# Two chained transformer blocks on one NeuronCore: the first modulation in column tiles of TensorE, constant-tile products spread behind four of its sums

## The chip, the cores and the metric

The kernel runs on one core of a Trainium2 chip. The metric is device time in microseconds of one execution, as the median of several runs. The engines are TensorE (PE in the profile, its weight loads PEld), VectorE (DVE), ScalarE (ACT), GpSimd (POOL) and SyncE (SP, which here only issues DMAs).

## What is computed

Two residual blocks over a sequence of 512 tokens of width 1024. The part that matters here is the head of the first block: a conditioning vector `c` (1024 values) is multiplied with `w_ada`, and the six parts of the result shift, scale and gate the two halves of the block. The first two parts, shift and scale, are needed before anything else can be multiplied:

```python
mod = c @ w_ada[layer] + b_ada[layer]
sh_a, sc_a, gt_a, sh_m, sc_m, gt_m = jnp.split(mod, 6, axis=-1)
h = modulate(rmsnorm(x, g_mix[layer]), sh_a, sc_a)   # rmsnorm(x) * (1 + sc_a) + sh_a
z = h @ w_in[layer]
```

Everything else (three kinds of attention, two feed-forward parts, a state-space mixer) comes after `z` and isn't touched.

## The kernel before

The activations lie transposed, features on the 128 partitions and the 512 tokens along the free axis: eight channel tiles of 128x512. All large products are made from rounded halves: each operand is split into a high part (`hh`, `wh`) and a low part (`hl`, `wl`), and three matmuls of the type fp32r (`wh·hh`, `wh·hl`, `wl·hh`) give one product. Plain f32 matmuls are used for small sums; each of those is two matmul instructions in the trace.

The program doesn't issue instructions at once. It records operations through `Rec`, and `Plan.schedule` (a list scheduler) then decides the order on each engine from estimated costs (`Plan.price`) and estimated DMA landings. Each engine takes, among the operations that are ready by the estimate, the one recorded first. On TensorE one rule is added: the estimate counts 0.2 us (`SWITCH`) for a change between tile shapes, and if the first candidate has another tile shape than the last matmul, a ready one of the same shape is preferred as long as it was recorded within the next 120 operations (`STAY`). The chip then runs each engine's list strictly in that order.

The start of the kernel goes like this:

- `warm(30)` issues 30 products of a constant tile `wt` with itself (128x512, fp32r), which nobody reads. They keep TensorE active while the first loads land.
- SP loads the eight tiles of `x` (`xT`), then the modulation's weights. For each channel tile `j` four DMAs bring `aw[j, 0..3]` (256 KB each), which hold `w_ada` for eight blocks `k` of 128 inputs and 256 outputs: 128 for the shift, 128 for the scale of channel tile `j`. Between them go the first pieces of `w_in` (`wr0` to `wr3`, 512 KB each).
- `SumSq` and `rstd_sb` make the row norm `R0`: squares on ACT, sums on DVE, four sums over partitions on TensorE, a power on POOL, a transpose that spreads it on TensorE (`T<-ident,rs`), a copy on ACT.
- `ada0_vec(j)` multiplies five of the eight blocks on DVE: one `tensor_scalar` and four `scalar_tensor_tensor` of 128x256 that accumulate into `aacc`. `ada0_sum(j)` does the other three on TensorE, with the weight block as the stationary operand and one column of `c` as the moving one (`S<-vec,aw`), and adds the column sums of `aacc` with a column of ones (`S<-ones,aacc`). Both accumulate in one PSUM bank; then ACT writes the shift (`mod`) and DVE the scale (`ca`).
- `h_tile(j)` makes the modulated tile: DVE multiplies `xT` with `ca` and `R0`, ACT adds the shift and rounds (`hh`), DVE makes the rest (`hl`).
- The first product, job 0 (`linT4`), accumulates four output tiles at once in four PSUM banks (two of tag `mm`, one `O`, one `S`). For each `k` from 0 to 7 it runs `start_step(k)`, which loads weights for tile `k + 5` and makes sum and modulated tile `k + 1`, and then 12 matmuls of 128x512 with tile `k`: 96 matmuls in all.
- After `ada0_vec(0)` stands `warm(18)`: 18 more products of the constant tile. A copy of a piece of `aacc` into `wt` just before makes them wait for that accumulation.

The tag `S` has three PSUM banks. One is an output bank of job 0 for its whole length, so two sums of the modulation can be under way at a time.

Of the kernel before, what the change touches and what calls it, by code (L numbers as in the profile page):

```python
# [10 lines left out]
F32 = mybir.dt.float32  # L11
F32R = mybir.dt.float32r
I32 = mybir.dt.int32
AF = mybir.ActivationFunctionType
OP = mybir.AluOpType
# [35 lines left out]
class Plan:  # L51
# [78 lines left out]
    def price(self, o, name, out, aps):  # L130


        free = lambda x: x.free_size() if callable(x.free_size) else x.free_size
        n = max([free(x) for x in aps]) if aps else 1
        ps = any(x.space == PSUM for x in aps)
        o.port, o.mode = False, None
        if name == "dma_start":
            sz = 4
            for d in out.shape:
                sz *= d  # L140
            o.nbytes = sz
            return 0.6 if o.eng == "POOL" else 0.06
        if o.eng == "PE":
            l, r = o.a[1], o.a[2]
            m, cut = free(l), lambda v: 32 if v <= 32 else 64 if v <= 64 else 128
            o.mode = (cut(l.ap[0][1]), 128 if name == "transpose" or r.dtype == F32R else cut(m))
            if name == "transpose":
                return 0.108
            if r.dtype == F32R:
                return max(0.11, free(r) / 2400.0 + 0.0136)  # L150
            return 2 * max(0.111 if m > 64 else 0.055 if m > 32 else 0.03,
                           (free(r) / 1200.0 + 0.005) * (1.0 if m > 32 else 0.4))
        if o.eng == "ACT":
            c = n / 1200.0 + (0.052 if ps else 0.093)
            if name == "activation" and (hasattr(o.kw.get("scale"), "tensor") or hasattr(o.kw.get("bias"), "tensor")):
                c += 0.093
            if o.kw.get("accum_out") is not None:
                c += 0.093
            return c
        ins = [x for x in aps if x is not out and x is not o.kw.get("accum_out")]  # L160
        big = [x for x in ins if free(x) > 8 and x.space != PSUM]
        two = name in ("tensor_scalar", "tensor_copy") and not ps
        if o.eng == "DVE":
            if name == "memset":
                return 0.01 + n / 960.0
            o.port = len(big) > 1 or (two and len(big) == 1)
            c = 0.069
            if name in ("tensor_scalar", "scalar_tensor_tensor"):
                c += 0.06 * sum(free(x) == 1 for x in ins)
            return c + n / (1920.0 if two else 960.0)  # L170
        if name == "memset":
            return 0.04 + n / 1200.0
        o.port = True
        if name == "tensor_copy":
            return 0.06 + n / 1040.0
        return 0.1 + n / 355.0 if name == "tensor_scalar" else 0.95 if n <= 8 else 0.15 + n / 475.0
# [347 lines left out]
def tile_kernel(ctx: ExitStack, tc: tile.TileContext, A, out):  # L524
    nc = tc.nc
    plan = Plan(nc)
    act, dve, pe, gp, sp = (Rec(plan, e) for e in ("ACT", "DVE", "PE", "POOL", "SP"))
# [21 lines left out]
    def nm(s):  # L549
        uid[0] += 1  # L550
        return f"{s}_{uid[0]}"

    def slot(dt=F32, name="a"):
        return plan.tile(ar, NA, [128, T], dt, "a", nm(name))
# [8 lines left out]
    def bank(tag):  # L563
        n = {"S": 3, "O": 1}.get(tag, 2)
        return plan.tile(psp[tag], n, [128, T], F32, tag, nm(tag))
# [7 lines left out]
    def mm(o, l, r, start, stop):  # L573
        pe.matmul(o, l, r, start=start, stop=stop, skip_group_check=True)
# [15 lines left out]
    def V(name):  # L590
        a, b = VEC[name]
        return vec[:, a:b]

    ones = cst.tile([128, 1], F32, name="ones")
# [3 lines left out]
    mod = cst.tile([128, 48], F32, name="mod")  # L598
    ca = cst.tile([128, 32], F32, name="ca")
# [52 lines left out]
    def rstd_sb(acc, n, tag="T"):  # L652
        p = spread(rstd_of(acc, n, tag), tag)
        R = slot(F32, "R")
        act.copy(R, p)
        return R
# [119 lines left out]
    cT = V("c")  # L776
# [127 lines left out]
    def comp_mlp(which):  # L904
        def body(ids):
# [54 lines left out]
    z = lambda j, ev: linT([wi[j, 0], wi[j, 1]], 4, 8, H1, ev)  # L960
    linT4([[wi[j, i] for i in range(2)] for j in range(2)], 4, 8, H1, [z_evac("kcvc"), z_evac("kskw")],
          pre=lambda k: start_step(k))
    z(4, z_evac("q")(0))
    beside([A["w_ck1"][i] for i in range(4)], comp_mlp("k"), 8.0)
# [484 lines left out]
    wt = slot(F32R, "warm")  # L1449
# [3 lines left out]
    def warm(n):  # L1453

        for _ in range(n):
            mm(wp, wt[:, 0:128], wt, True, True)
    warm(30)
    for i in range(8):
        x1[i] = slot(F32, "xT")
        sp.dma_start(x1[i], A["xT"][i])  # L1460
    aw = {}

    def ada0_load(j):
        for i in range(4):
            aw[j, i] = slot(F32, "aw")
            sp.dma_start(aw[j, i], A["w_ada0"][j, i])

    acc0 = {}
    KD = 5

    def ada0_vec(j):

        acc = slot(F32, "aacc")
        w = lambda k: aw[j, k // 2][:, 256 * (k % 2):256 * (k % 2) + 256]
        dve.tensor_scalar(acc[:, 0:256], w(0), cT[:, 0:1], None, op0=OP.mult)
        for k in range(1, KD):
            dve.scalar_tensor_tensor(acc[:, 0:256], w(k), cT[:, k:k + 1], acc[:, 0:256], op0=OP.mult, op1=OP.add)
        acc0[j] = [(w(k), cT[:, k:k + 1]) for k in range(KD, 8)] + [(acc, ones)]

    def ada0_sum(j):  # L1480
        p = bank("S")
        for i, (x, v) in enumerate(acc0[j]):
            for m in range(2):
                mm(p[:, m:m + 1], x[:, 128 * m:128 * m + 128], v, i == 0 and m == 0, i == len(acc0[j]) - 1)
        act.activation(mod[:, j:j + 1], p[:, 0:1], AF.Identity, bias=V("b_ada")[:, j:j + 1])
        dve.scalar_tensor_tensor(ca[:, j:j + 1], p[:, 1:2], ca[:, 16 + j:17 + j], V("g_mix")[:, j:j + 1], op0=OP.add,
                                 op1=OP.mult)

    def h_tile(j):
        t = x1.pop(j)  # L1490
        dve.scalar_tensor_tensor(t, t, ca[:, j:j + 1], R0, op0=OP.mult, op1=OP.mult)
        h1.append(hilo(t, bias=mod[:, j:j + 1], name="h"))
        later.flush()
# [10 lines left out]
    ss0 = SumSq(8)  # L1504
    for i in range(8):
        ss0.add(x1[i])
    ada0_vec(0)
    dve.tensor_copy(wt[:, 0:8], acc0[0][-1][0][:, 0:8])
    warm(18)
    R0 = rstd_sb(ss0, 1024)  # L1510
    ada0_sum(0)
    ada0_vec(1)
    h_tile(0)
    W.need(1)
    later.flush()

    def start_step(k):
        if k + 5 < 8:
            ada0_load(k + 5)
        if k == 2:  # L1520
            W.need(3)
        if k == 4:
            for t, n in ((DT, "dt"), (MK, "mk"), (CS, "cs")):
                sp.dma_start(t, A[n])
            for g in range(2):
                sp.dma_start(NBC[g], A["nbc"][g])
        if k + 1 < 8:
            ada0_sum(k + 1)
            if k + 2 < 8:
                ada0_vec(k + 2)  # L1530
            h_tile(k + 1)
        yield 0.0

# [435 lines left out]
    p = bank("T")  # L1969
# [310 lines left out]
```

## Time and profile before

| | |
|---|---|
| median of 3 runs | 1442.59 us (1439.56, 1442.59, 1442.77) |
| the profiled execution | 1439.8 us, of which the span of its instructions is 1437.7 us |
| mean granted TensorE clock | 0.991 |
| busy time | PE 98%, PEld 82%, DVE 65%, ACT 43%, POOL 10% of the span |

A matmul's shown duration contains its way through the array, so consecutive ones overlap; the cost of a matmul in a row of them is the distance from start to start. "PEclk" is the clock that TensorE was granted, as a share of 2.4 GHz (0.5 is 1.2 GHz). A line of the timeline or the groups has the shape `start, duration, engine, line, operation, out<-in, tile, shape, count [idle before <- what ended it]`; all instructions have line 377, the recording helper, so the names tell them apart. `128*32` is a matmul that uses 128 rows and 32 columns of the array.

### The profile page before, as it was taken

What the parts mean: (1) busy time and instruction counts of PE and PEld (TensorE: products, weight loads), DVE (VectorE), ACT (ScalarE), POOL (GpSimd) and SP (SyncE); (2) the same over time, 40 slices, a digit from 0 to 9 for tenths busy, and PEclk for the clock granted to TensorE, in tenths of its full rate; (3) what the DMA queues carried; (4) which work ended last, traced back from release to release, by engine and by line L of the source; (5) the groups of instructions that cost most, each with busy time, mean ns of one, the idle gap of its engine ahead of it and who ended that gap; (6) DMA issues with size and microseconds to landing.
All of it is one profiled execution on the core that took longest, in us unless ns stands there. A gap on an engine that the chain in (4) does not pass through costs nothing.

```text
span 1437.7 us, 19122 instructions
## 1 busy us (share of the span) xinstructions
PE 1402.6 (98%) x7152; PEld 1173.3 (82%) x7152; DVE 937.2 (65%) x1830; ACT 614.5 (43%) x1065; POOL 137.3 (10%) x177
## 2 busy tenths in 40 slices
PE   9999999999999999999999999998999999999996
PEld 7889888877888888888888887886888888888885
DVE  6867777779887886946544656778776534553544
ACT  3435567667643442323324533767443312321322
POOL 1010001200000000000213121244300000000000
PEclk9999999999999999999999999998999999999999
DMA  9583453542264233244446666241233333333221
GB/s 365 183 304 102 141 156 138 161 140 59 82 200 145 59 110 97 88 126 131 142 149 189 216 231 133 70 133 48 75 93 97 92 105 98 88 103 117 88 59 59
DMA packets 73372, 185.81 MB, mean 129 GB/s; under 512 B 17048, under 2 KB 17896, under 8 KB 73280
## 3 DMA queue, kind: packets, MB, share of 16 engines
q1 hardware_dynamic: 64192, 159.67, 36.0%
q0 software_dynamic: 7552, 22.97, 5.0%
q10 hardware_dynamic: 1536, 1.95, 0.4%
q8 instruction: 56, 0.92, 0.3%
q14 instruction: 36, 0.29, 0.1%
HBM read 165.41 MB, written 19.67 MB: 129 GB/s over the span
## 4 chain that ended last, share of the span: by engine, by line
PE 84%; DVE 6%; ACT 3%; DMA 2%; issue 2%; POOL 2%; SPq 0%; DVEq 0%; POOLq 0%; ACTq 0%
PE mm L377 70%; PE T L377 5%; PE S L377 5%; PE O L377 3%; POOL x L377 1%; DMA adaw<-in_w_ada 1%; DVE sb L377 1%; DVE pl L377 1%; ACT sb L377 1%; DVE o L377 1%; ACT wh L377 1%; DVE xt L377 0%; DVE adacc L377 0%; DMA aw<-in_w_ada 0%; SPq L377 0%
## 5 line engine op out<-in xcount | busy, mean ns | idle before, releaser
L377 ACT CAST wh<-wr 128x1024 fp32r<-128x1024 f32 x209 | 219.8, 1051 | 380.5 <-PE mm L377 321.0
L377 PE MATMUL mm<-hh,wh 128*128 128x512 f32 x880 | 353.3, 402 | 3.7 <-ACT fm L377 1.9
L377 DVE TENSOR_TENSOR wl<-wr,wh 128x1024 fp32r<-128x1024 f32 x206 | 258.3, 1254 | 135.6 <-ACT wh L377 128.8
L377 PE MATMUL mm<-hl,wh 128*128 128x512 f32 x880 | 345.7, 393 | 0.0
L377 PE MATMUL mm<-hh,wl 128*128 128x512 f32 x880 | 345.4, 393 | 0.0
L377 PEld LDWEIGHTS mm<-hh,wl 128*128 128x128 f32 x880 | 165.3, 188 | 34.9 <-issue 0.2
L377 PEld LDWEIGHTS mm<-hh,wh 128*128 128x128 f32 x880 | 165.3, 188 | 34.4 <-issue 2.5
L377 PEld LDWEIGHTS mm<-hl,wh 128*128 128x128 f32 x880 | 165.7, 188 | 29.9
L377 PE MATMUL mm<-fh,wl 128*128 128x512 f32 x416 | 162.0, 390 | 0.0
L377 PE MATMUL mm<-fh,wh 128*128 128x512 f32 x416 | 162.0, 390 | 0.0
L377 PE MATMUL mm<-fl,wh 128*128 128x512 f32 x416 | 161.9, 390 | 0.0
L377 PEld LDWEIGHTS mm<-fh,wh 128*128 128x128 f32 x416 | 78.1, 188 | 16.5 <-issue 0.2
L377 PEld LDWEIGHTS mm<-fh,wl 128*128 128x128 f32 x416 | 78.1, 188 | 16.3
L377 PEld LDWEIGHTS mm<-fl,wh 128*128 128x128 f32 x416 | 78.1, 188 | 16.2
L377 ACT ACTIVATE sb<-sb,st 128x512 f32<-128x512 f32 (+3 forms) x128 | 71.5, 559 | 28.9 <-DVE st L377 26.7
L377 DVE TENSOR_TENSOR pl<-T,ph 128x384 fp32r<-128x384 f32 (+1 forms) x96 | 56.5, 595 | 21.5 <-ACT ph L377 16.0
L377 PE MATMUL T<-ident,sb 128*128 128x128 f32 x320 | 55.2, 280 | 5.9 <-DVE pl L377 2.8
L377 ACT CAST ph<-T 128x384 fp32r<-128x384 f32 (+1 forms) x96 | 48.1, 509 | 24.3 <-PE T L377 23.4
L377 DVE CUSTOM_DVE_ANT_0 sb<-S,nb 128x256 f32<-128x256 f32 (+2 forms) x96 | 44.9, 484 | 15.6 <-PE S L377 15.3
L377 PEld LDWEIGHTS T<-ident,sb 128*128 128x128 f32 x320 | 39.5, 143 | 18.1 <-issue 4.0
L377 DVE TENSOR_TENSOR swg<-mm,R 128x512 f32<-128x512 f32 x21 | 14.5, 691 | 60.9 <-PE mm L377 60.9
L377 ACT ACTIVATE sw<-swg 128x512 f32<-128x512 f32 x22 | 13.9, 631 | 83.4 <-DVE swg L377 83.4
(376 smaller groups left out, 2357.0 us busy)
## 6 DMA issues: line engine op xcount, KB each, us to landing
wr<-in_w_fc SPq DMA_DIRECT2D x64, 512.0 KB, 3.6
wr<-in_w_in SPq DMA_DIRECT2D x48, 512.0 KB, 4.0
wr<-in_w_gu SPq DMA_DIRECT2D x44, 512.0 KB, 3.6
adaw<-in_w_ada POOLq DMA_DIRECT2D x32, 512.0 KB, 5.0
wr<-in_w_down SPq DMA_DIRECT2D x22, 512.0 KB, 3.5
aw<-in_w_ada SPq DMA_DIRECT2D x32, 256.0 KB, 6.6
wr<-in_w_out SPq DMA_DIRECT2D x16, 512.0 KB, 3.9
rec<-srec SPq DMA_DIRECT2D x28, 256.0 KB, 6.5
```

The costliest lines, as they stand in the source:

```text
L377: fn(*o.a, **o.kw)
```

## The change

All eight blocks of a channel tile's modulation go to TensorE, and DVE's share of it goes away. The roles of the operands are swapped: the stationary operand is now a 128x32 tile `cz[:, k]` that has block `k` of `c` in its first column and zeros in the other 31, and the weight block (128x256) moves. The result is written to 32 of the 128 partitions of the bank, in a column tile of the array given by `k % 4`; blocks 4 to 7 accumulate on blocks 0 to 3. So four partial sums stand on partitions 0, 32, 64 and 96. ACT copies the bank to `acc`, and two f32 products with the column of ones add the partitions (and turn the result to one value a partition), as before for `aacc`. The estimate for matmuls with at most 32 stationary columns is lowered from 0.4 to 0.25 of a whole matmul. The second run of 18 constant-tile products goes away; 7, 7, 5 and 4 of them stand behind the sums of channel tiles 0, 1, 2 and 3, each set waiting for that sum's `acc`; the first run has 34 instead of 30. The recorded place of each `ada0_sum` is unchanged.

```diff
             return 2 * max(0.111 if m > 64 else 0.055 if m > 32 else 0.03,
-                           (free(r) / 1200.0 + 0.005) * (1.0 if m > 32 else 0.4))
+                           (free(r) / 1200.0 + 0.005) * (1.0 if m > 32 else 0.25))
...
-    warm(30)
+    warm(34)
...
-    acc0 = {}
-    KD = 5
-
-    def ada0_vec(j):
-
+    cz = slot(F32, "cz")[:, 0:256].rearrange("p (k c) -> p k c", k=8)
+    gp.memset(cz, 0.0)
+    dve.tensor_copy(cz[:, :, 0], cT)
+
+    def ada0_sum(j):
+
+
+        p = bank("S")
+        for k in range(8):
+            w = aw[j, k // 2][:, 256 * (k % 2):256 * (k % 2) + 256]
+            r = 32 * (k % 4)
+            mm(p[r:r + 32, 0:256], cz[:, k], w, k < 4, k >= 4)
         acc = slot(F32, "aacc")
-        w = lambda k: aw[j, k // 2][:, 256 * (k % 2):256 * (k % 2) + 256]
-        dve.tensor_scalar(acc[:, 0:256], w(0), cT[:, 0:1], None, op0=OP.mult)
-        for k in range(1, KD):
-            dve.scalar_tensor_tensor(acc[:, 0:256], w(k), cT[:, k:k + 1], acc[:, 0:256], op0=OP.mult, op1=OP.add)
-        acc0[j] = [(w(k), cT[:, k:k + 1]) for k in range(KD, 8)] + [(acc, ones)]
-
-    def ada0_sum(j):
-        p = bank("S")
-        for i, (x, v) in enumerate(acc0[j]):
-            for m in range(2):
-                mm(p[:, m:m + 1], x[:, 128 * m:128 * m + 128], v, i == 0 and m == 0, i == len(acc0[j]) - 1)
-        act.activation(mod[:, j:j + 1], p[:, 0:1], AF.Identity, bias=V("b_ada")[:, j:j + 1])
-        dve.scalar_tensor_tensor(ca[:, j:j + 1], p[:, 1:2], ca[:, 16 + j:17 + j], V("g_mix")[:, j:j + 1], op0=OP.add,
+        act.copy(acc[:, 0:256], p[:, 0:256])
+        for m in range(2):
+            mm(p[:, 256 + m:257 + m], acc[:, 128 * m:128 * m + 128], ones, True, True)
+        if j < 4:
+            dve.tensor_copy(wt[:, 0:8], acc[:, 0:8])
+            warm((7, 7, 5, 4)[j])
+        act.activation(mod[:, j:j + 1], p[:, 256:257], AF.Identity, bias=V("b_ada")[:, j:j + 1])
+        dve.scalar_tensor_tensor(ca[:, j:j + 1], p[:, 257:258], ca[:, 16 + j:17 + j], V("g_mix")[:, j:j + 1], op0=OP.add,
                                  op1=OP.mult)
...
-    ada0_vec(0)
-    dve.tensor_copy(wt[:, 0:8], acc0[0][-1][0][:, 0:8])
-    warm(18)
     R0 = rstd_sb(ss0, 1024)
     ada0_sum(0)
-    ada0_vec(1)
     h_tile(0)
...
             ada0_sum(k + 1)
-            if k + 2 < 8:
-                ada0_vec(k + 2)
             h_tile(k + 1)
```

## Rows read from the trace of the kernel before

**Rows 1.** The page: busy time of each engine.

```profile
PE 1402.6 (98%) x7152; PEld 1173.3 (82%) x7152; DVE 937.2 (65%) x1830; ACT 614.5 (43%) x1065; POOL 137.3 (10%) x177
```

**Rows 2.** Windows: length, busy time by engine (instructions), PEclk, DMA share, GB/s.

```profile
14.20:21.10 6.90, 6.90 (x21) 5.64 (x22) 4.88 (x10) 2.35 (x3) 3.25 (x5) 0.52 1.04 395
...
22.20:25.40 3.20, 3.20 (x31) 3.18 (x29) 1.54 (x4) 1.46 (x3) 0.00 (x0) 1.00 1.04 395
25.40:57.20 31.80, 31.80 (x182) 27.38 (x182) 27.57 (x55) 10.51 (x17) 0.00 (x0) 1.00 0.81 298
```

**Rows 3.** Timeline, PE alone, from the start to the first real product.

```profile
1.50 9.93 PE L377 MATMUL T<-warm 128*128 128x512 f32 x30 [1.50 <-DVE warm L377]
...
12.15 1.03 PE L377 MATMUL T<-ones,ssq 128*128 128x1 f32 x8
...
15.19 7.18 PE L377 MATMUL T<-warm 128*128 128x512 f32 x18
22.22 0.60 PE L377 MATMUL T<-ident,rs 128*128 128x128 f32 x4
...
25.47 0.71 PE L377 MATMUL mm<-hh,wh 128*128 128x512 f32 x2
```

**Rows 4.** Groups by form: the modulation's products; busy us, mean ns, idle before.

```profile
L377 PE MATMUL S<-vec,aw 128*128 128x1 f32 x96 | 11.9, 244 | 0.5 <-DMA aw<-in_w_ada 0.5
...
L377 DVE SCALAR_TENSOR_TENSOR aacc<-aw,vec,aacc 128x256 f32<-128x256 f32 x32 | 14.8, 478 | 0.2
...
L377 DVE TENSOR_SCALAR aacc<-aw,vec 128x256 f32<-128x256 f32 x8 | 2.6, 348 | 0.1
```

**Rows 5.** Timeline, PE: one whole sum between products of job 0.

```profile
44.95 0.39 PE L377 MATMUL S<-hh,wl 128*128 128x512 f32 x1
...
46.88 0.49 PE L377 MATMUL mm<-hh,wh 128*128 128x512 f32 x1
...
47.21 0.40 PE L377 MATMUL mm<-hl,wh 128*128 128x512 f32 x1
```

**Rows 6.** Timeline, PE: four column tiles at 128 columns (state-space tables, much later).

```profile
721.42 0.39 PE L377 MATMUL mm<-fl,wh 128*128 128x512 f32 x1
...
721.65 0.39 PE L377 MATMUL mm<-fh,wl 128*128 128x512 f32 x1
...
721.97 0.43 PE L377 MATMUL T<-PCr,blk 128*32 128x128 f32 x8
...
722.54 0.50 PE L377 MATMUL mm<-fh,wh 128*128 128x512 f32 x1
...
722.88 0.40 PE L377 MATMUL mm<-fl,wh 128*128 128x512 f32 x1
```

**Rows 7.** Windows of 0.06 us inside that block: PE, PEld busy (instructions in flight).

```profile
722.00:722.06 0.06, 0.06 (x4) 0.06 (x8) 0.00 (x0) 1.00 0.00 0
722.06:722.12 0.06, 0.06 (x8) 0.06 (x11) 0.00 (x0) 1.00 0.00 0
...
722.18:722.24 0.06, 0.06 (x12) 0.06 (x8) 0.00 (x0) 1.00 0.00 0
```

**Rows 8.** Groups by form: steps between a sum and its products.

```profile
L377 ACT COPY ye<-T 128x256 f32<-128x256 f32 x8 | 2.6, 372 | 0.8 <-PE T L377 0.6
...
L377 POOL TENSOR_TENSOR rs<-ms,mhalf 128x4 f32<-128x4 f32 x1 | 1.2, 1187 | 13.1 <-DVE ms L377 13.1
...
L377 DVE SCALAR_TENSOR_TENSOR xT<-xT,ca,R 128x512 f32<-128x512 f32 x6 | 4.5, 745 | 3.0 <-ACT R L377 3.0
L377 ACT ACTIVATE hh<-xT,mod 128x512 fp32r<-128x512 f32 x6 | 4.3, 721 | 6.4 <-DVE xT L377 6.4
```

**Rows 9.** Timeline: loads of the last three tiles, cast of the third piece.

```profile
25.16 10.47 SPq L377 DMA_DIRECT2D aw<-in_w_ada  x12
...
31.31 1.05 ACT L377 CAST wh<-wr 128x1024 fp32r<-128x1024 f32 x1 [1.74 <-DMA wr<-in_w_in]
```

**Rows 10.** The page's DMA issues: count, KB each, us to landing.

```profile
aw<-in_w_ada SPq DMA_DIRECT2D x32, 256.0 KB, 6.6
```

More of the change, by code (lines that the diff above doesn't have):

```diff
@@ L1466, in ada0_load @@
             sp.dma_start(aw[j, i], A["w_ada0"][j, i])
-    acc0 = {}
-    KD = 5
-    def ada0_vec(j):
-        acc = slot(F32, "aacc")
-        w = lambda k: aw[j, k // 2][:, 256 * (k % 2):256 * (k % 2) + 256]
-        dve.tensor_scalar(acc[:, 0:256], w(0), cT[:, 0:1], None, op0=OP.mult)
-        for k in range(1, KD):
-            dve.scalar_tensor_tensor(acc[:, 0:256], w(k), cT[:, k:k + 1], acc[:, 0:256], op0=OP.mult, op1=OP.add)
-        acc0[j] = [(w(k), cT[:, k:k + 1]) for k in range(KD, 8)] + [(acc, ones)]
+    cz = slot(F32, "cz")[:, 0:256].rearrange("p (k c) -> p k c", k=8)
+    gp.memset(cz, 0.0)
+    dve.tensor_copy(cz[:, :, 0], cT)
     def ada0_sum(j):
         p = bank("S")
-        for i, (x, v) in enumerate(acc0[j]):
-            for m in range(2):
-                mm(p[:, m:m + 1], x[:, 128 * m:128 * m + 128], v, i == 0 and m == 0, i == len(acc0[j]) - 1)
-        act.activation(mod[:, j:j + 1], p[:, 0:1], AF.Identity, bias=V("b_ada")[:, j:j + 1])
-        dve.scalar_tensor_tensor(ca[:, j:j + 1], p[:, 1:2], ca[:, 16 + j:17 + j], V("g_mix")[:, j:j + 1], op0=OP.add,
+        for k in range(8):
+            w = aw[j, k // 2][:, 256 * (k % 2):256 * (k % 2) + 256]
+            r = 32 * (k % 4)
+            mm(p[r:r + 32, 0:256], cz[:, k], w, k < 4, k >= 4)
+        acc = slot(F32, "aacc")
+        act.copy(acc[:, 0:256], p[:, 0:256])
[6 more added lines that the diff above has]
+        dve.scalar_tensor_tensor(ca[:, j:j + 1], p[:, 257:258], ca[:, 16 + j:17 + j], V("g_mix")[:, j:j + 1], op0=OP.add,
                                  op1=OP.mult)
```

## The prediction

> **What bounds the kernel now.** I read the page first: TensorE is busy for 98% of the span [rows 1], so a change is worth what it takes off TensorE's own sequence, or off a wait that TensorE shows. The windows of the start come next. From the first real product to the end of job 0, at 25.4 to 57.2 us, TensorE is busy all 31.8 us at full clock, and VectorE 27.6 [rows 2]: VectorE is crowded, yet TensorE waits for nothing. So the 17.4 us that VectorE loses (14.8 and 2.6) [rows 4] give nothing by themselves. Ahead of that stretch the timeline shows what is poor: 18 constant products take 7.18 us, 0.40 each, because the clock fell to half (0.52 on average) [rows 2, 3], where neighbouring products of that size stand 0.23 apart at full clock [rows 6]. The spread of `R0` stands behind them on TensorE, at 22.22, and the first real product starts at 25.47 [rows 3]. So the change is costed on TensorE alone, from the start to the end of job 0 at 57.2.
>
> **One sum.** Before: from the product ahead of a sum to the second one behind it 47.21 - 44.95 = 2.26 us [rows 5]; less two pitches of 0.23 that leaves 1.80 us for 16 instructions, 0.11 each; twelve of the sixteen are the weight products, of which there are 96 in all [rows 4]. The same reading of the column-tile block gives 722.88 - 721.65 - 0.46 = 0.77 us for 16 instructions of 128 columns [rows 6]. Inside it the instructions in flight go up in fours, 4, 8, 12, some 0.11 us apart [rows 7]: four tiles do run side by side, four rounds make 0.43, and 0.34 goes to entering and leaving the tile shape. The new sum also has 8 products of two instructions, with 256 columns: rounds of 0.21, so 0.77 + 0.43 = 1.20 us. The two products with ones stay, 4 of 16 instructions or 0.45. Together **1.65 against 1.80 us**, 0.15 saved a sum. Bounds: 1.3 where two sums run back to back and share the entry; above, the case that the tiles don't run side by side at 256 columns, which is a rival.
>
> The Trainium skill speaks against this step: "TensorE: Matmul & The Clock Gate", Part 3, The mechanism, says that a weight load overlaps with running matmuls only if it goes to other row groups, and column tiles share all rows. The rows contradict it: loads and matmuls of several column tiles are in flight together [rows 7]. By the rule 16 passes of 0.21 would stand in a row; that is the last rival.
>
> **The new wait.** `acc` must leave PSUM before the two products with ones: a copy of 128x256 on ACT, 0.37 us by its nearest row [rows 8], and a handover either way. Behind the waiting products stand, in TensorE's list, the constant products or job 0's; on VectorE the copy into `wt` waits for `acc` and for the last constant products, with the low parts of the weights and `xT` queued behind. From the products with ones to job 0's first product with that tile it is then scale, 0.75 (`xT`) and 0.72 (`hh`), some 2.5 us with handovers, and about 3.2 for `hl` [rows 8]. Nothing but other ready work on TensorE covers that.
>
> **Constant products.** Four more at the start: 4 x 0.23 = 0.9, so they end at 12.3, not 11.4 (1.50 + 9.93 [rows 3]). Of the later ones 18 go and 23 come; at full clock 23 x 0.23 = 5.3 us against 7.18.
>
> **Walk of TensorE after the change.** To 12.3 the constant products; then the eight norm sums (0.9 [rows 3]) and sixteen column products of tiles 0 and 1 as their weights land (two blocks, with changes of shape): 15.0. POOL's power (1.19 [rows 8]) holds the spread until about 15.9; products with ones and spread to 16.4; seven constant products to 18.0; the rest of sum 1 to 18.7. `R0`'s copy, `xT`, the cast of the first weight piece (1.05 [rows 9]) and `hh` follow the spread one by one, which gives the first real product at about **19.1 instead of 25.5**. Left then: 96 x 0.23 = 21.8 of products, 16 x 0.23 = 3.6 of constant ones, 0.45 for the ones of sum 1, six sums at 1.65 = 9.9: 35.7, to 54.8. Waits: about 0.6 at 19 to 21, where `hl` and sum 1's copy are late. A second comes from the planner's preference for the tile shape that it is in: a sum in column tiles is put off while products of job 0 are ready, so two sums come together behind them and job 0 runs dry for the 2.5 us chain; counting through, about 0.6 near 46. Back-to-back pairs give back 2 x 0.3. Job 0 ends at **55.5, 1.7 us earlier**.
>
> Do the loads allow it? The last tile's loads are issued until 25.16 + 10.47 = 35.6 [rows 9] and land 6.6 later [rows 10], at 42.2; the walk needs them at 45. The third weight piece comes at 31.3 [rows 9], its first use is at about 41. SP's order changes little, POOL gains one memset at the start, under the first loads. So loads cover the change, by 3 us; a larger gain than that would begin to be cut. Behind job 0 the same gap and the same loads follow, all released by its end, so the shift should pass through.
>
> **The rest.** No later operation changes, but the planner's estimated times do, by a few us, and the lower estimate for narrow matmuls shifts the state-space tables by about 1 us of estimate; near ties in a list of 19,000 instructions can fall otherwise. TensorE is idle for 35 us in the span (1437.7 - 1402.6 [rows 1]); one or two waits of 1 to 2 us appearing or going is what I allow, with either sign.
>
> **The sum.** The profiled execution took 1439.8 us, span 1437.7; minus 1.7 is 1438.1. The shown runs lie at 1439.6 and at 1442.6 to 1442.8, their median 1442.59, and minus 1.7 that is 1440.9. I take 1440.0, between the two, nearer the median.
>
> **Rivals.**
> - *TensorE never waits and the sums pair up.* The planner then places sums so that four pairs share an entry (4 x 0.34) and neither wait of 0.6 is there: from 12.3, 0.9 + 0.6 spread + 8 x 1.65 - 1.4 + 5.3 + 21.8 = 40.4, end at 52.7, 4.5 us earlier, 1437.2 from the same base (1441.7). For it: VectorE has room for every chain. Against: the first product can't start before about 19, and the `S` banks allow two sums at once.
> - *The clock falls all the same* (slower than before). In the trace it had fallen by 14.2, after only 2.8 us of narrow work behind the dense products, and came back about 21.1, after 5.9 us of constant products at half speed [rows 2, 3]. After the change the thin stretch goes from 12.3 to 16.4, with 16 wider column products in it. If it falls there, the first 14 constant products cost 14 x 0.17 = 2.4 more and the products among them some 0.8: instead of -1.7 it is +1.5, 1443.2. It decides if the clock is low over more than about 3.5 us of that stretch. Against: at 22.2 to 25.4 the trace has 3.2 us of equally thin work and keeps its clock [rows 2].
> - *The gain is lost or doubled further on*, by other orders: 1436 to 1446.
> - *The change doesn't shorten anything*: job 0's end is set by landings after all, near 57: 1441.7.
> - *Column tiles one after the other at 256 columns*: 16 x 0.21 = 3.4 instead of 0.85, eight times: +20, 1460.
>
> **Chances.** The forecast 0.42 (its own range 1438 to 1443), no waits 0.27, clock 0.14, other orders 0.10, loads 0.04, serial tiles 0.03. The base itself is uncertain by 1.5 us either way. The range runs from 1435.5, for the no-wait case with a good order, to 1444.5, for the clock; outside are the serial tiles and the ends of the other orders. A measurement of this kernel can tell about 0.3%, 4.3 us. Faster by more than that needs the no-wait case, or the forecast with a good order: 0.31. Slower by more than that: the clock's case with a bad order, part of the other orders, serial tiles: 0.08. Between: 0.61.
>
> **What would show it.** Right: the first `hh,wh` product near 19; column blocks of about 1.2 us with fours in flight; job 0's last product near 55.5; the constant products 0.23 apart behind each of the four sums, at granted clock 1.0. Wrong: column products over 0.3 us apart; PEclk 0.5 between 15 and 22; TensorE idle ahead of job 0's products for more than 1.2 us in total; job 0 early, but a later stage longer than before.

## The result, and the profile after

| | before | after |
|---|---|---|
| median | 1442.77 us, 15 runs (1438.37 to 1450.48) | 1450.15 us, 15 runs (1447.27 to 1455.28) |
| the profiled execution (its span) | 1439.8 us (1437.7) | 1455.28 us (1453.5) |
| mean granted TensorE clock | 0.991 | 0.983 |

The ratio after to before is **1.0051, 95% interval 1.0037 to 1.0066**: 5.3 to 9.5 us slower. The prediction was 1440.0 us, with a range from 1435.5 to 1444.5; the result lies outside it, on the other side of no change. The chance given to slower by over 0.3% was 0.08.

The page's busy line, against [rows 1]: VectorE has lost 11 us and TensorE is busy 9.4 us longer, with 41 matmuls more in 7193.

```profile
PE 1412.0 (97%) x7193; PEld 1174.7 (81%) x7193; DVE 925.9 (64%) x1794; ACT 617.1 (42%) x1073; POOL 135.8 (9%) x178
```

The timeline of TensorE after the change, against [rows 3] (start, duration, engine, line, operation, out<-in, tile, shape, count, idle before and what ended it):

```profile
1.50 9.95 PE L377 MATMUL T<-warm 128*128 128x512 f32 x34 [1.50 <-DVE warm L377]
11.38 1.06 PE L377 MATMUL S<-aw,cz 128*32 128x256 f32 x12
...
14.91 0.63 PE L377 MATMUL T<-ident,rs 128*128 128x128 f32 x4
...
17.88 0.73 PE L377 MATMUL mm<-hh,wh 128*128 128x512 f32 x2
...
20.63 1.78 PE L377 MATMUL T<-warm 128*128 128x512 f32 x7
...
26.65 1.50 PE L377 MATMUL S<-aw,cz 128*32 128x256 f32 x24
31.97 1.05 PE L377 MATMUL S<-ones,aacc 128*128 128x1 f32 x8 [3.83 <-ACT aacc L377]
33.04 2.50 PE L377 MATMUL T<-warm 128*128 128x512 f32 x5
35.47 1.51 PE L377 MATMUL S<-aw,cz 128*32 128x256 f32 x16
...
46.71 1.93 PE L377 MATMUL S<-aw,cz 128*32 128x256 f32 x32
48.58 1.17 PE L377 MATMUL S<-ones,aacc 128*128 128x1 f32 x8
49.86 1.07 PE L377 MATMUL S<-aw,cz 128*32 128x256 f32 x16
52.00 0.73 PE L377 MATMUL mm<-hh,wh 128*128 128x512 f32 x2 [1.07 <-ACT hh L377]
...
60.68 0.39 PE L377 MATMUL S<-hh,wl 128*128 128x512 f32 x1
63.02 0.50 PE L377 MATMUL mm<-hh,wh 128*128 128x512 f32 x1 [1.95 <-ACT fm L377]
```

To 28 us the start goes better than forecast: the first real product stands at 17.88, where it stood at 25.47 before [rows 3]. Then TensorE stands still for 3.83 us, from 28.1 to 31.97, because the products with ones of tiles 2 and 3 wait for ScalarE's copy `aacc`. Behind it the five constant products take 0.49 us each (35.47 - 33.04, by five) instead of 0.23. Job 0's last product comes at 60.68; in the trace of before it came at 56.81. The windows show the same stretch, against [rows 2] (length, busy time of PE, PEld, DVE, ACT and POOL with instruction counts, PEclk, DMA share, GB/s):

```profile
17.90:28.10 10.20, 10.20 (x67) 7.06 (x67) 4.08 (x7) 2.12 (x4) 0.00 (x0) 1.00 1.05 394
28.10:31.90 3.80, 0.05 (x4) 0.00 (x0) 0.22 (x1) 1.29 (x3) 0.00 (x0) 1.00 1.02 394
31.90:37.00 5.10, 5.01 (x30) 3.11 (x30) 4.48 (x9) 2.38 (x6) 0.00 (x0) 0.67 1.05 387
37.00:60.90 23.90, 22.71 (x140) 17.24 (x140) 11.72 (x19) 7.94 (x15) 0.00 (x0) 1.00 0.57 206
```

In the second window TensorE, VectorE and GpSimd are idle or nearly so, ScalarE is busy for 1.29 us at its end, and the DMA engines run at full share: everything hangs on a transfer. Which one is seen in ScalarE's timeline:

```profile
21.36 0.72 ACT L377 ACTIVATE hh<-xT,mod 128x512 fp32r<-128x512 f32 x1 [0.59 <-DVE xT L377]
30.61 1.04 ACT L377 CAST wh<-wr 128x1024 fp32r<-128x1024 f32 x1 [8.53 <-DMA wr<-in_w_in]
31.56 0.64 ACT L377 COPY aacc<-S 128x256 f32<-128x256 f32 x2
```

ScalarE works its list in order. Behind `hh` of tile 1 stands the cast of the third weight piece, and behind that the copies of sums 2 and 3. The cast waited 8.53 us for its load. The piece's load was issued by SP behind the tile loads:

```profile
23.62 1.98 SPq L377 DMA_DIRECT2D wr<-in_w_in  x2
```

The third piece is the first of the two. It took some 7 us to land, with the transfers issued before it still under way; the page's median for such a piece is 4.1 us. The copies had nothing to do with that load, and the piece's own first user is the fifth step of job 0, whose products begin at 43.90, 13 us later.

How far the loss is carried can be read from POOL's loads for the next modulation, which wait for job 0's successors. The first of them, before and after:

```profile
77.00 0.53 POOL L377 DMA_DIRECT2D adaw<-in_w_ada  x1 [59.55 <-ACT ct L377]
...
82.44 0.53 POOL L377 DMA_DIRECT2D adaw<-in_w_ada  x1 [65.54 <-ACT ct L377]
```

At the eighth such load (99.51 before) the changed kernel is 5.0 us late. Laid side by side, the products of the two traces are 5.5 us apart at 280 us and 6.6 to 6.9 between 340 and 840 us, after a further fall of the clock at 289. The profiled run, the slowest of the fifteen, lost another 9 us between 860 and 1010 us, of which more below.

### The profile page after: what moved, and what is told of

The parts are those of the page before. It is cut to its first block, busy times and chain, and to the rows that moved or that the text cites. A ratio compares the mean times of both kernels' runs of the same rounds, so it can differ in the third digit from the quotient of the medians.

```text
span 1453.5 us, 19180 instructions
## 1 busy us (share of the span) xinstructions
PE 1412.0 (97%) x7193; PEld 1174.7 (81%) x7193; DVE 925.9 (64%) x1794; ACT 617.1 (42%) x1073; POOL 135.8 (9%) x178
## 3 DMA queue, kind: packets, MB, share of 16 engines
q10 hardware_dynamic: 1536, 1.95, 0.4%
## 4 chain that ended last, share of the span: by engine, by line
PE 83%; DVE 7%; DMA 4%; ACT 3%; issue 2%; DVEq 0%; SPq 0%; POOLq 0%; POOL 0%; ACTq 0%
PE mm L377 70%; PE T L377 5%; PE S L377 4%; PE O L377 3%; DMA adaw<-in_w_ada 1%; DMA wr<-in_w_in 1%; DVE sb L377 1%; DMA aw<-in_w_ada 1%; DVE pl L377 1%; ACT sb L377 1%; ACT wh L377 1%; DVE o L377 1%; DVE xt L377 0%; DVE sr L377 0%; DVE wl L377 0%
## 5 line engine op out<-in xcount | busy, mean ns | idle before, releaser
L377 PEld LDWEIGHTS mm<-fh,wl 128*128 128x128 f32 x416 | 78.1, 188 | 16.4
L377 DVE CUSTOM_DVE_ANT_0 sb<-S,nb 128x256 f32<-128x256 f32 (+2 forms) x96 | 45.0, 484 | 22.7 <-PE S L377 21.8
L377 DVE TENSOR_TENSOR swg<-mm,R 128x512 f32<-128x512 f32 x21 | 14.5, 692 | 61.2 <-PE mm L377 61.2
```

The source lines that it names most:

```text
L377: fn(*o.a, **o.kw)
```

## The experiments

Each kernel was timed in five rounds beside the kernel before. "First" and "last" are the first and the last product of job 0 (us); "waits" are TensorE's between them, of 0.3 us or more; "low" is where the granted clock begins to fall to half before 70 us; "late by" is the distance of POOL's eighth `adaw` load from its 99.51 of before.

| kernel | first | last | waits | low | late by | ratio to before, 95% interval |
|---|---|---|---|---|---|---|
| before | 25.47 | 56.81 | none | 14.4 | - | - |
| after | 17.88 | 60.68 | 3.83, 1.07 | 33.0, 63.7 | 5.0 | 1.0051 [1.0037, 1.0066] |
| e1 | 18.36 | 56.42 | none | 60.2 | 0.5 | 1.0019 [1.0005, 1.0034] |
| e2 | 18.35 | 60.35 | 0.33, 1.41 | 54.2 | 2.4 | 1.0017 [1.0001, 1.0034] |
| e3 | 26.98 | 58.42 | none (2.79 ahead of it) | 23.8, 61.3 | 2.4 | 1.0012 [0.9998, 1.0026] |
| e4 | 20.16 | 58.76 | 0.99, 0.79 | 33.8, 61.1 | 2.1 | 1.0007 [0.9988, 1.0025] |
| e5 | 18.52 | 57.85 | 1.18, 0.47 | 61.2 | 3.2 | 1.0007 [0.9985, 1.0028] |
| e6 | 19.48 | 59.11 | 0.33, 1.87, 0.49 | 49.9 | 1.7 | 1.0018 [1.0004, 1.0032] |
| e7 | 18.98 | 56.06 | 0.71, 1.32 | none | -1.8 | 1.0003 [0.9988, 1.0019] |
| e8 | 19.48 | 57.88 | 0.44, 0.31, 2.10 | 50.8 | 0.2 | 1.0006 [0.9990, 1.0022] |
| e9 | 18.56 | 56.73 | 0.39, 0.48 | none | -1.2 | 1.0013 [0.9994, 1.0031] |
| e10 | 18.71 | 56.08 | 0.37, 1.19 | 59.2 | 0.0 | 1.0012 [0.9995, 1.0030] |
| e12 | 26.39 | 59.16 | none | 15.6 | 2.1 | 0.9988 [0.9969, 1.0006] |
| e13 | 18.22 | 54.66 | 0.49, 1.98 | 57.4 | -0.9 | 1.0007 [0.9988, 1.0026] |

**e1: the copy on VectorE.** The copy no longer stands in the list in which the cast waits.

```diff
-        act.copy(acc[:, 0:256], p[:, 0:256])
+        dve.tensor_copy(acc[:, 0:256], p[:, 0:256])
```

> One line of the changed kernel: the bank goes to acc by VectorE instead of ScalarE. Queue theory: in the changed kernel TensorE stood still for 3.83 us (28.1 to 32.0) since the copies of sums 2 and 3 stand on ScalarE behind the cast of the third weight piece, which waits for its load until 30.6; with the copies on VectorE, ahead of the low parts, that wait is gone, job 0's last product ends before 57 us instead of 61.1, and the time is 1437 to 1442, ratio to before 0.996 to 1.000. Work theory (the column products and nine more constant products are themselves what costs): job 0 still ends at 60 to 61 and the ratio stays near 1.005. Clock theory (the loss is made by falls of the granted clock later on, whatever the start does): job 0 ends earlier, the ratio stays above 1.003.

The third cast still waits for its load, until 30.75, but the copies no longer wait with it: that of sum 2 starts at 27.46 on VectorE. Only tile 2's `hh` is still held, until 31.70 behind the cast, and TensorE has other work meanwhile. ScalarE and VectorE in e1:

```profile
30.75 1.05 ACT L377 CAST wh<-wr 128x1024 fp32r<-128x1024 f32 x1 [2.01 <-DMA wr<-in_w_in]
...
27.46 0.42 DVE L377 COPY aacc<-S 128x256 f32<-128x256 f32 x1 [1.71 <-PE S L377]
```

The standstill and the low clock behind it are gone, job 0 ends 4.26 us earlier than in the changed kernel, and the ratio falls from 1.0051 to 1.0019. So the place of the copy in ScalarE's list is what cost most. The gain that was expected (0.996 to 1.000) didn't come, though: the interval lies above 1, so e1 is still slower than before.

**e2: the piece loaded earlier.** `W.dma(3)` moves ahead of the loads of tiles 3 and 4; order and engines of all else stay.

```diff
-    for j in (2, 3, 4):
+    ada0_load(2)
+    W.dma(3)
+    for j in (3, 4):
         ada0_load(j)
-    W.dma(3)
```

> The changed kernel with the third and fourth weight piece loaded ahead of the modulation's tiles 3 and 4 instead of behind them; the copies stay on ScalarE. Queue theory: the cast finds its data by about 25 us, the 3.83 us of standstill shrink to under 1.5, job 0 ends at 57 to 59 (tiles 3 and 4 land 2.7 us later than before, which can cost a little), ratio 0.998 to 1.003. Work theory: ratio 1.005, job 0 at 60 to 61.

The cast now starts at 26.00 and the 3.83 us are gone, but they come back in smaller pieces: a column block of sum 3 begins late and runs through the arrival of its own weights, and there is a wait for `hh` near 53. TensorE in e2:

```profile
28.07 2.57 PE L377 MATMUL S<-aw,cz 128*32 128x256 f32 x16 [0.33 <-DMA aw<-in_w_ada]
...
53.41 0.73 PE L377 MATMUL mm<-hh,wh 128*128 128x512 f32 x2 [1.41 <-ACT hh L377]
```

A block of 16 column products takes 1.07 undisturbed; this one took 2.50 (to the products at 30.57). Job 0's last product is at 60.35, nearly as late as in the changed kernel and later than the 57 to 59 expected, while POOL's eighth `adaw` load is only 2.4 us late. The DMA engines are at full share all the while (1.01 to 1.05 in e2 from 20 to 40 us), so what is loaded sooner pushes the tiles later. The ratio falls to 1.0017, as far as in e1.

**e3 and e4: one part of the change alone.** e3 has the column sums with the constant products of before (30, then 18 behind sum 0). e4 has the sums of before with the constant products of the change (34, then 7, 7, 5, 4).

```diff
-    warm(34)
+    warm(30)
...
-        if j < 4:
-            dve.tensor_copy(wt[:, 0:8], acc[:, 0:8])
-            warm((7, 7, 5, 4)[j])
...
+    ada0_mul(0)
+    dve.tensor_copy(wt[:, 0:8], acc0[0][1][:, 0:8])
+    warm(18)
```

> The column-tile sums alone, with the constant products as before: 30 at the start and 18 behind the first acc, ahead of the spread. Queue theory: the 18 fall to half clock again and the first real product starts near 23 to 25; the copies of sums 1 and 2 stand ahead of the third cast, only sum 3 behind it, so the standstill is under 1.5 us, job 0 ends at 57 to 59 and the ratio is 0.999 to 1.004. Work theory with the column products as the cost: ratio 1.004 or more without a standstill that names the copy.

> The constant products alone as in the change (34 at the start; 7, 7, 5 and 4 behind sums 0 to 3), the sums as before on VectorE and TensorE. Queue theory: there is no copy on ScalarE, so nothing waits for the third cast; the first real product starts near 18 to 20, the five more products and sums cost what they cost, VectorE becomes crowded; job 0 ends at 55 to 58, ratio 0.996 to 1.001. Work theory with the constant products as the cost: ratio 1.003 or more.

Neither part alone is a gain or a loss that can be measured. In e3 the 18 products ran at full clock (14.68 to 18.87, 0.23 each), where half was expected. The first product is late all the same (26.98, expected 23 to 25), because the planner put half of tile 3's column products, the 49th to 56th, ahead of it, where TensorE waited for their weights:

```profile
23.63 0.97 PE L377 MATMUL S<-aw,cz 128*32 128x256 f32 x4 [1.86 <-DMA aw<-in_w_ada]
25.53 1.07 PE L377 MATMUL S<-aw,cz 128*32 128x256 f32 x4 [0.93 <-DMA aw<-in_w_ada]
```

In e4 the first product comes 5.3 us earlier than before and job 0 ends 2 us later, at 58.76 (55 to 58 expected). TensorE's waits are only 1.8 us, but the constant products that follow sums 1 to 3 are now between real ones, and the clock fell at 33.8 and behind job 0.

**e5: no preference for the tile shape.** The planner counts the modulation's column products as full-width ones, so it has no reason to put sums off and join them.

```diff
-            o.mode = (cut(l.ap[0][1]), 128 if name == "transpose" or r.dtype == F32R else cut(m))
+            o.mode = (cut(l.ap[0][1]), 128 if name == "transpose" or r.dtype == F32R else 128 if free(r) == 256 and m == 32 else cut(m))
```

> The changed kernel, but the planner counts the new products as whole-array ones, so its preference for the tile shape that it is in doesn't see them. Order theory (the preference put sum 2 off behind two tiles of job 0, and so its copy behind the third cast): the copy of sum 2 now stands ahead of that cast, only that of sum 3 behind it; the 3.83 us of standstill shrink to under 1.5, job 0's last product at 56 to 58, ratio to before 0.999 to 1.003. Rival (the preference saves changes of shape, and without it these cost more than it gives): job 0 at 59 or later, ratio 1.003 or more.

The sums stand one by one. The copy of sum 2 comes ahead of the third cast, that of sum 3 behind the fourth, at 33.27, and 1.18 us of the wait are left.

**e6, e7 and e8: fewer constant products.** Behind sum 0 seven, behind the others none. e6 has this and the copy of e1; e7 that and the planner of e5; e8 only the fewer constant products, with the copy on ScalarE.

```diff
-        if j < 4:
+        if j < 1:
             dve.tensor_copy(wt[:, 0:8], acc[:, 0:8])
-            warm((7, 7, 5, 4)[j])
+            warm(7)
```

> The copy on VectorE (as in the first experiment) and constant products behind sum 0 alone: 7, 0, 0, 0. Theory that constant products behind sums 1 to 3 stand on TensorE's path and cover nothing: 16 x 0.23 = 3.7 us less than the first experiment, job 0's last product at 53 to 54.5 instead of 56.4, ratio 0.996 to 0.999, granted clock still 1.0 from 21 to 56. Rival (they keep the clock): a stretch at 0.5 between 18 and 40 us, job 0 at 56 or later, ratio 1.001 or more. Rival (loads bound the start): TensorE waits for the weights of tiles 3 to 7, job 0 at 55.5 to 56.5.

> The experiment before (copy on VectorE, 7 constant products behind sum 0 only), and the planner counts the new products as whole-array ones. Order theory: sums come one at a time as their loads land, job 0's last product at 52.5 to 54.5, ratio 0.995 to 0.999. If changes of shape cost more than the preference's pairs: 0.5 to 1.5 us later than the experiment before.

> The changed kernel with its copy on ScalarE, but constant products behind sum 0 alone. In the planner's order the copies of sums 2 and 3 now stand ahead of the third cast, since TensorE reaches these sums earlier by its estimate. Order theory: no standstill over 1.5 us, 16 fewer constant products, job 0's last product at 53.5 to 56, ratio 0.997 to 1.001. If the constant products were not what put the copies behind the cast: job 0 at 57 or later.

All three end job 0 later than expected (59.11, 56.06 and 57.88). e8 leaves the copy where it was; yet the wait is gone, since with other estimated times the copies happen to be listed ahead of the third cast (27.89 against 31.18). Its job 0 ends late for another reason, a wait of 2.10 us for `hh` at 51 and the fall of the clock with it. e6 shows the same trap on VectorE: the copy of a later sum is listed behind two low parts `wl` of the next job's weights.

```profile
46.91 2.35 DVE L377 TENSOR_TENSOR wl<-wr,wh 128x1024 fp32r<-128x1024 f32 x2
49.17 0.21 DVE L377 SCALAR_TENSOR_TENSOR ca<-S,ca,vec 128x1 f32<-128x1 f32 x1
49.30 0.41 DVE L377 COPY aacc<-S 128x256 f32<-128x256 f32 x1
```

TensorE waits 1.87 us for that copy and the clock falls behind it, at 49.9. e7's job 0 ends ahead of before's (56.06), as e1's did, and e7 is the first whose later work runs early (-1.8); in the median that can't be told from no change.

**e9: the planner told of the later landing.** One number of the estimate is changed, no operation: loads expected between 17 and 45 us are counted 3 us later.

```diff
-                end = dma + 0.9
+                end = dma + (3.9 if 17.0 < dma < 45.0 else 0.9)
```

> The changed kernel, with one number of the planner's estimate changed: loads that it expects to land between 17 and 45 us are counted 3 us later, about what the trace of the changed kernel shows for the third weight piece (expected near 27, landed 30.6). No operation is added or taken away. In the planned order ScalarE's copies of the sums of tiles 2 and 3 then stand ahead of the cast of that piece. Theory (the cast that waits for its load holds the copies, 3.8 us): TensorE's waits before 50 us come to 1 us at most, job 0's last product is at 56 to 58 us (60.7 in the changed kernel), the ratio to the kernel before is 0.999 to 1.003. Rival (the column sums and the constant products cost the time themselves, or the clock does): the last product stays near 60, the ratio at 1.004 or above.

TensorE and ScalarE in e9, to be laid beside the lines above of the changed kernel:

```profile
26.75 1.93 PE L377 MATMUL S<-aw,cz 128*32 128x256 f32 x32
...
27.88 0.37 ACT L377 COPY aacc<-S 128x256 f32<-128x256 f32 x1 [5.13 <-PE S L377]
28.75 0.37 ACT L377 COPY aacc<-S 128x256 f32<-128x256 f32 x1 [0.49 <-PE S L377]
29.51 0.26 ACT L377 ACTIVATE mod<-S,vec 128x1 f32<-128x1 f32 x1 [0.39 <-DVE ca L377]
31.62 1.05 ACT L377 CAST wh<-wr 128x1024 fp32r<-128x1024 f32 x1 [1.85 <-DMA wr<-in_w_in]
```

TensorE reaches the column products of tiles 2 and 3 at the same time as in the changed kernel (26.75 and 26.65). The cast starts 1 us later than there, the copies 3.7 us earlier. The waits left are 0.48 us or shorter, the clock doesn't fall before 890 us, and job 0 ends at 56.73, 3.95 us earlier than in the changed kernel and level with before. The ratio is 1.0013, and its interval lies wholly below that of the changed kernel. With the same operations on the same engines, order alone makes the 5 us. The edit can move other operations too; what it shares with e1, e2 and e8 is that the copies no longer stand behind a cast that waits.

**e10, e12 and e13: the later landing with the other edits, and as a control.** e10 is e7, e12 the kernel before, e13 is e8, each with e9's edit.

> The three mends of e7 (acc copied by VectorE, constant products behind the first sum only, no tile-shape preference for the modulation's columns) with the later landing estimate of e9 as well. Theory (what is left after e7 is casts and low parts queued ahead of work that is ready): the wait of 1.3 us for hh near 53 shrinks, job 0's last product is at 54 to 56 us, the ratio is 0.996 to 1.000. Rival (the loads themselves bound job 0): its last product stays near 56, a wait for aw or a cast is in the place of the one removed, the ratio is 1.000 to 1.002.

> Control: the kernel before with the later landing estimate alone. Theory: its sums don't go through ScalarE, so nothing of the modulation stands behind a cast there; job 0's last product stays within 1 us of 56.8 and the ratio is 0.999 to 1.001. Rival (a better landing estimate is worth time by itself, whatever the change): the ratio is under 0.998.

> The changed kernel with the later landing estimate of e9, and the constant products behind the first sum only (7, 0, 0, 0 instead of 7, 7, 5, 4): 16 constant products fewer, which are 3.7 us at 0.23 each. In e9 TensorE waits for only 1.5 us before the end of job 0 at 56.7. Theory (the constant products of tiles 1 to 3 lie on TensorE's path and no longer fill any wait): job 0's last product is at 53 to 55 us, the ratio to the kernel before is 0.996 to 1.000. Rival (job 0 is bound by the chain of sum, scale and modulated tile and by the loads, and the constant products only fill that time): the last product stays at 55.5 to 57, with waits 2 to 4 us longer in all, and the ratio is as in e9.

e10 gains nothing over e7: a wait of 1.19 for `hh` stays near 53. The control's ratio, 0.9988, can't be told from no change, so no worth of the estimate by itself is shown. Its trace missed what was expected of it: job 0 ended 2.35 us later than in the profile of before. Of this 1.31 us is not the edit's: the first eight weight loads took 6.31 us to issue where they took 4.83, and the first sum's weight products began at 13.24 instead of 11.93, before any load whose estimate was changed. The rest is order: the weight products of the third sum, which before has ahead of its first real product (24.13), now stand behind it, and TensorE waits 0.81 us for `hh` in their place. One look at the start is thus no better than some 1 to 2 us. In e13 16 constant products fewer (3.7 us) end job 0 2.07 us earlier; the rest comes back as a wait:

```profile
52.03 0.73 PE L377 MATMUL mm<-hh,wh 128*128 128x512 f32 x2 [1.98 <-ACT hh L377]
...
54.66 0.39 PE L377 MATMUL S<-hh,wl 128*128 128x512 f32 x1
57.00 0.50 PE L377 MATMUL mm<-hh,wh 128*128 128x512 f32 x1 [1.95 <-ACT fm L377]
57.34 0.55 PE L377 MATMUL mm<-hl,wh 128*128 128x512 f32 x1
57.69 0.63 PE L377 MATMUL mm<-hh,wl 128*128 128x512 f32 x1
58.11 0.63 PE L377 MATMUL mm<-hh,wh 128*128 128x512 f32 x1
```

Of the 2.15 us by which job 0 ends earlier than before's, 0.9 are left at the eighth `adaw` load: after the gap behind job 0 the products stand 0.43 apart, which is half the clock; in the kernel before the same gap is followed by products 0.23 apart. No version beats the kernel before by what can be measured, and e1, e2 and e6 are slower by what can (their intervals lie above 1).

## Why the prediction was wrong

**Right: the first product and the sums.** The forecast had the spread at 15.9 and the first product at 19.1; they came at 14.91 and 17.88. Some 0.9 of the 1.2 us is luck: in this profile the constant products went over to full clock at 5.7 us, in before's at 7.6, so 34 of them ended at 11.4 instead of the 12.3 that was worked out. (In the profiles of the variants this point lies between 4.5 us, in e10, and 6.7, in e3.) A sum's 16 column products were put at 1.20 us with entering and leaving the tile shape. Read as the prediction read its rows, from the product ahead to the second one behind less two pitches of 0.23, a block alone in e5 took 31.18 - 29.52 - 0.46 = 1.20:

```profile
29.52 0.39 PE L377 MATMUL S<-hh,wl 128*128 128x512 f32 x1
29.84 1.07 PE L377 MATMUL S<-aw,cz 128*32 128x256 f32 x16
30.84 0.50 PE L377 MATMUL mm<-hh,wh 128*128 128x512 f32 x1
31.18 0.40 PE L377 MATMUL mm<-hl,wh 128*128 128x512 f32 x1
```

Two sums together took 1.87 from the first column product to the first product with ones (46.71 to 48.58 in the changed kernel). Four column tiles do run side by side at 256 columns, as the block of 128 columns had shown [rows 6, 7]. The prediction held that against the Trainium skill, "TensorE: Matmul & The Clock Gate", Part 3, The mechanism, by which loads overlap only between row groups. As the prediction read that rule, the 32 products of the pair, at 0.21 us one after the other, would take 6.7 us; they took 1.87, so it fails here.

**Right: loads of the tiles, and nearly so the orders behind the start.** In the changed kernel TensorE doesn't wait for a tile's weights. Behind 110 us TensorE's operations come in the order of before but for two products near 758 us, ScalarE's but for two operations (758 and 940 us), VectorE's but for seven (between 217 and 774 us) and SP's but for one load (787 us). So there is little ground for "other orders further on", though no run takes these few apart.

**Wrong: the waits, 1.2 us in the sum, 4.9 in the trace.** This is the step that failed. The part on the new wait named what is queued behind the waiting instructions on TensorE and on VectorE, and gave ScalarE's copy its duration of 0.37 [rows 8]. It didn't ask what stands *ahead* of the copy in ScalarE's list. The row was there: the third cast at 31.31, which waits 1.74 us for its DMA [rows 9]. The prediction read that row as a matter of the piece's own use ("its first use is about 41") and found ten us to spare. But a cast that waits holds whatever is listed behind it. Before, that cost nothing, since the sums went from VectorE to TensorE and ScalarE had only `mod` and `hh` to do. The change put a step of every sum into that list and had the sums of tiles 2 and 3 due at 27 to 28, ahead of the landing.

That the copy was listed behind the cast is the planner's doing, and could have been worked out: by its formula (bytes by a fixed rate behind the transfers issued before) the piece lands near 27, as the expectation of e9 has it, and it landed at 30.6. Moving the copy (e1), loading the piece earlier (e2), correcting the landing (e9), or merely other times (e8) each take the 3.83 us away.

**Partly right: the clock rival.** It was placed at 12.3 to 16.4, where the granted clock in fact stayed at 1.00 (the first stretch at half behind it begins at 33.0). It fell behind the standstill instead and made the five constant products and the column block there 1.7 us longer (5 x 0.26, and 1.45 for 1.07). So the rival's sign was right, but its cause was a wait that the sum didn't have.

**The sum again.** The forecast's end of job 0 was 55.5 (its last product at some 55.3) and the trace has 60.68 for the last product, 5.4 later: -1.2 for the earlier first product, +3.7 for waits (4.9 against 1.2), +1.7 for the clock, and 1.2 that I can't place in single rows; the 0.6 taken off for joined sums is in it. (The 21.8 for 96 products is right; the pitch is 0.227, which the sum wrote as 0.23.) The loss then passes through the gap behind job 0, as forecast for the gain: at the next job's first product it is 3.9 us (63.02 against 59.15). There the clock falls once more, at 63.7, and by POOL's eighth load the loss is 5.0.

**Wrong as well: that a repaired order would gain.** e9 and e13 have what the forecast described, waits of 1.1 to 2.7 us in all, and end job 0 at 56.7 and 54.7, around the forecast 55.5. Yet in the median neither is faster than before. A gain of 1 to 2 us is below what these runs tell: the intervals are some 0.18% (2.6 us) to either side. The profiles also show where a lead goes, which the prediction had named as a sign of being wrong ("job 0 early, but a later stage longer than before"). SP's loads of `ud` and of `w_out` mark the ends of one such stage, in before and then in e9:

```profile
859.96 2.42 SPq L377 DMA_DIRECT2D ud<-u  x3
...
1010.75 6.92 SPq L377 DMA_DIRECT2D wr<-in_w_out  x2
```

```profile
858.46 2.42 SPq L377 DMA_DIRECT2D ud<-u  x3
...
1012.75 6.92 SPq L377 DMA_DIRECT2D wr<-in_w_out  x2
```

e9 comes 1.5 us ahead of before and leaves 2.0 behind it; e13 goes from 1.1 ahead to 2.4 behind, e7 from 2.1 ahead to 2.9 behind.

**What stays open.** Why that stage, 860 to 1010 us, is longer. It takes 150.8 us in before and 148.1 in the control; in the changed kernel and its eleven variants, the two with one part alone (e3, e4) among them, it takes 153.5 (e1) to 160.0 (the changed kernel). Between 860 and 990 us each of these profiles has one or two stretches of low clock, and in all but e1 and e6 one begins between 893 and 904 us; before has one at 875 and the control none. The order of the operations there is nearly that of before. But this is one profile of each kernel, before's was taken from a run 3 us below its median and the changed kernel's from one 5 us above, and before's own runs differ by 12 us. So it isn't settled whether this loss comes from the shift of the start, from the few changed places in the order, or from the run.

## What to carry to other kernels

Where a step moves to another engine, read that engine's list *ahead* of it: a waiting instruction there holds everything behind it, so a cheap copy (0.37 us) can cost its neighbour's transfer (3.83 us). In a scheduled program the order comes from estimated landings; compare them with the landings in the trace before trusting an order, and look at each cast that waits for a DMA as a gate for the work listed behind it. Bringing the first product forward by 7.6 us was worth nothing here by itself. In e9 it comes 6.9 us earlier than before and job 0 ends level with before: 3.7 us of that are the sixteen constant products that now stand behind it, about 1.1 are waits. Where e13 takes these constant products out, 2.1 us come back as an earlier end and the rest as a wait for `hh`; that the loads and the chain of sum, scale and modulated tile set the end in general isn't shown.

## What the hardware showed that was not expected

Two column-tiled f32 sums in a row cost less than their parts. In e8 the pair at 34.41, read as the single block above, took 36.62 - 34.10 - 0.46 = 2.06 us against 2 x 1.20, so 0.34 us of a block goes to entering and leaving the tile shape, as the prediction had it from the block of 128 columns. And the granted clock, which in the kernel before survived the gap of 1.95 us behind job 0, fell behind a gap of the same length (1.94 to 1.95) in the changed kernel and in six others (e1, e3, e4, e5, e10 and e13); in e7 and the control it didn't. Behind the gap of 1.28 us in e2, e6, e8 and e9 it never fell. What tells e7, the control and before from the seven isn't clear from the rows.
